# A two-layer streaming encoder: row tiles kept in one pool from the mixer to the next half-step, the embedding through the weight ring, raw buffers by stage, one down block reordered

## The chip, the cores and the metric

The kernel runs on one core of one Trainium2 chip. Its time is the time of one execution on the device in microseconds (us). The engines are named as in the profile: PE is the matrix engine (TensorE) and PEld its weight loads, DVE is VectorE, ACT is ScalarE, POOL is GpSimd, and SP only issues DMAs (its queue appears as SPq). PE runs at one of two clocks, 1.2 or 2.4 GHz; the profile gives the granted clock of a stretch as a share of the higher one.

## The reference, cut to what matters

The kernel computes two consecutive encoder layers on 512 tokens of width 1024, all in fp32. LN is a layer norm over the 1024 channels, alpha = (2*DEPTH)^(1/4).

```
for each of DEPTH = 2 layers:
  x <- LN(alpha*x + 0.5*SwiGLU_1(x))                      # first half-step, D_FF = 2816
  x <- LN(alpha*x + W_out(sum_b sigmoid(G_b x) * (W_b y_b)))   # four mixers y_A..y_D
  x <- LN(alpha*x + 0.5*SwiGLU_2(x) + sigmoid(x W_pg) * (p[i] W_p))   # second half-step + per-layer embedding

def swiglu(x, w_up, w_down):
    a, b = jnp.split(x @ w_up, 2, axis=-1)
    return (jax.nn.silu(a) * b) @ w_down
```

p[i] is an embedding of 256 numbers per token, one for each layer; the kernel gets it transposed, as pT.

## The kernel before, in words

The 512 tokens are four **row tiles** of 128 (i = 0 to 3, NT = 4). The running residual is z0 to z3, one [128, 1024] tile for each row tile; the operand of the matmuls is its transpose, which `norm` makes on PE (tiles lnT) and splits.

**Precision.** Every matmul is made of three passes (`mm3`, lines 163 to 165): each operand is split into a high part and a low rest (`split`, lines 177 and 178: ACT casts the high part, DVE subtracts it from the source). A "group" below is one `mm3`, three matmuls. A weight tile so needs four steps (`weights`): SP issues a DMA of 512 KB into a raw tile named `stage`, ACT casts `whi`, DVE subtracts `wlo`, and PE reads both. Finished pairs have six slots. Raw tiles come from `stage()`: four buffers in the pool `ring`, and four more in the pool `more` while the pool `tt` is open; `stage()` alternates between the two. `norm` takes raw tiles for its intermediate sums as well (`sums`).

**Stages of a layer.** The first half-step (`ffn`, which = 1) goes over 22 blocks of D_FF in four chunks (6, 6, 6 and 4). `unit` computes the up product of a block with seven products of block sums in place of eight; the operands of these are th and tl, which live in the pool `tt`. `down` then adds a chunk's blocks into z. Then `mix` runs the four mixers, gates and merges them into `mg`, multiplies by the output weights (tiles wo), adds to z and normalises. The second half-step (`ffn`, which = 2) begins with `ple`: for each half of the channels, pw = p times the embedding weights (wple) and pg = x times the gate's (wpg), then the same up and down loops. The last chunk's down product is `down_last`: for each row tile and each half of the channels it goes over the block pairs pr, and after each row tile a `norm` is spawned. The norm after `down_last` of the first half-step and the mixer's norm also write z to DRAM (`scratch`, tiles xs), from where the next stage loads it again.

**Order.** PE's order is written out by hand: generators such as `norm` are woven into the main stream at estimated times (`Weave`), and PE executes them in that order. On ACT, DVE and SP the scheduler decides the order; each engine then goes strictly through its own list. So an instruction that waits holds up all that stands behind it on its engine, and a DMA that waits holds up all DMAs behind it on SP's queue.

Of the kernel before, what the change touches and what calls it, by code (L numbers as in the profile page):

```python
# [9 lines left out]
F32 = mybir.dt.float32  # L10
F32R = mybir.dt.float32r
I32 = mybir.dt.int32
AF = mybir.ActivationFunctionType
ALU = mybir.AluOpType
# [4 lines left out]
P = 128  # L19
D = 1024  # L20
KD = D // P
SEQ = 512
NT = SEQ // P
DEPTH = 2
# [16 lines left out]
class Weave:  # L41
# [25 lines left out]
    def spawn(self, gen):  # L67
        c = Chain(gen)
        self.chains.append(c)
        self.step(c)  # L70
        return c
# [8 lines left out]
class Trunk:  # L80
# [14 lines left out]
    def __init__(self, tc, ctx, t):  # L95
        self.tc, self.nc, self.t = tc, tc.nc, t
        pool = lambda *a, **k: ctx.enter_context(tc.tile_pool(*a, **k))
        self.const = pool(name="const", bufs=1)
        self.ring = pool(name="ring", bufs=1)
        self.small = pool(name="small", bufs=4)  # L100
        self.dram = pool(name="dram", bufs=1, space=DRAM)
        self.psum = pool(name="psum", bufs=8, space=PSUM)
        c = self.const
        self.xh = c.tile([P, KD, SEQ], F32R, tag="xh", name="xh")
        self.xl = c.tile([P, KD, SEQ], F32R, tag="xl", name="xl")
        self.ident = c.tile([P, P], F32, tag="ident", name="ident")
        self.mhalf = c.tile([P, 8], F32, tag="mhalf", name="mhalf")
        self.st, self.ln = {}, []
        self.tt, self.turn = None, False
        self.scratch = [self.dram.tile([P, D], F32, tag=f"xs{i}", name=f"xs{i}") for i in range(NT)]  # L110
        self.w = Weave()

# [5 lines left out]

    def stage(self):
        self.turn = not self.turn  # L120
        if self.tt is not None and self.turn:
            return self.more.tile([P, 1024], F32, tag="stage", name="stage", bufs=4)
        return self.ring.tile([P, 1024], F32, tag="stage", name="stage", bufs=4)

# [127 lines left out]
        self.th, self.tl = [p.tile([P, 4, HK, HT], F32R, tag=q, name=q) for q in ("th", "tl")]  # L252

    def close_tt(self):
        self.tt.close()
        self.tt = None

    def xop(self, c):

# [116 lines left out]
            v.tensor_scalar(s, s, -1.0, 0.5 * math.pi, op0=ALU.mult, op1=ALU.add)  # L376
            nc.scalar.activation(self.cos, s, AF.Sin)

    def load_res(self, z, src):
        for i in range(NT):  # L380
            self.load(z[i], src[i])

    def load_gb(self, g, b, l, which):
        self.load(g, self.t[f"ln{which}_g"][l].partition_broadcast(P))
# [4 lines left out]
            self.st[i] = self.small.tile([P, 2, 6], F32, tag="st", name="st", bufs=5)  # L389
        self.nc.vector.bn_stats(self.st[i][:, half, :], z[:, half * 512:(half + 1) * 512])  # L390

    def norm(self, z, i, g, b, last, blocks):
        nc = self.nc
        mv = self.small.tile([P, 2], F32, tag="mv", name="mv")
        nc.vector.bn_aggr(mv, self.st[i])
# [7 lines left out]
                nc.sync.dma_start(out=self.t["out"][i][:, c], in_=z[:, c])  # L403
        if last:
            return
        self.load(self.scratch[i], z)
        for j in range(2):
            yield 8.5 if j == 0 else 1.0
            ps = self.bank("lnT", [P, 4, P])
            for q in range(4):  # L410
                k = 4 * j + q
# [27 lines left out]
            self.mm3(ps[:, c0:c1], w[0][:, s], w[1][:, s], self.xh[:, k, c0:c1], self.xl[:, k, c0:c1],  # L439
                     k == 0, k == KD - 1)  # L440

    def ffn(self, l, which, res, last):
        nc, t = self.nc, self.t
        v = nc.vector
        up, dn = t[f"up{which}"][l], t[f"dn{which}"][l]
        pool = lambda n: self.tc.tile_pool(name=f"{n}{l}{which}", bufs=1, reuse_waits="tile")
        with pool("z") as zp:
            first_use = l == 0 and which == 1
            if first_use:
                scratch = zp.tile([P, D], F32, tag="z3", name="trig")  # L450
            z = []

            def load_rows():
                z.extend(zp.tile([P, D], F32, tag=f"z{i}", name=f"z{i}") for i in range(NT))
                self.load_res(z, res)

            if not first_use:
                load_rows()
            if which == 2:
                with pool("ple") as pp:  # L460
                    self.ple(l, z, pp, self.load_p(l, pp))
            with pool("ffn") as fp:
                self.ffn_body(l, which, last, fp, z, up, dn, load_rows, scratch if first_use else None)

    def ffn_body(self, l, which, last, fp, z, up, dn, load_rows, scratch):
        nc, t = self.nc, self.t
        v = nc.vector
        lead = 2 if which == 1 else 0
        alpha = ALPHA2 if which == 1 else None
        h = {}  # L470
# [28 lines left out]
        def down_last(k0, k1, g, b):  # L499
            prs = range(k0 // 2, k1 // 2)  # L500
            ws = {(pr, half): self.weights(dn[pr, half]) for half in range(2) for pr in prs}
            self.ln = []
            for i in range(NT):
                for half in range(2):
                    ps = self.bank(f"dn{i}")
                    for pr in prs:
                        w = ws[pr, half]
                        for j in range(2):
                            s, m = slice(i * P, (i + 1) * P), slice(j * 512, (j + 1) * 512)
                            self.mm3(ps, h[pr][:, 0, j, s], h[pr][:, 1, j, s], w[0][:, m], w[1][:, m],  # L510
                                     2 * pr + j == k0, 2 * pr + j == k1 - 1)
                    zs = z[i][:, half * 512:(half + 1) * 512]
                    v.tensor_tensor(zs, zs, ps, op=ALU.add)
                    self.stats(z[i], i, half)
                self.ln.append(self.w.spawn(self.norm(z[i], i, g, b, last, which == 2)))

        for ci, (k0, k1) in enumerate(CHUNKS):
            first, tail = ci == 0, ci == len(CHUNKS) - 1
# [19 lines left out]
                g, b = gb[:, 0, :], gb[:, 1, :]  # L538
                self.load_gb(g, b, l, 1 if which == 1 else 3)
            while tt < k1:  # L540
                if scratch is not None and tt == lead + 2:
                    self.constants(scratch)
                    load_rows()
                self.ready(*range(NT))
                cc, X, nb = self.unit(up[tt // 2], fp)
                finish(tt // 2, cc, (X, nb))
                tt += 2
# [11 lines left out]
            self.nc.vector.tensor_tensor(cc[:, q], cc[:, q], ps[2 * q + 1], op=ALU.mult)  # L559
        self.split(h[0][:, 0], h[0][:, 1], cc)  # L560

    def load_p(self, l, pp):
        ps_ = pp.tile([P, 2, SEQ], F32, tag="ps", name="ps_")
        ph = pp.tile([P, 2, SEQ], F32R, tag="ph", name="ph")
        pl = pp.tile([P, 2, SEQ], F32R, tag="pl", name="pl")
        self.load(ps_, self.t["pT"][l])
        self.split(ph, pl, ps_)
        return ph, pl

    def ple(self, l, z, pp, pt):  # L570
        nc, t = self.nc, self.t
        ph, pl = pt
        for half in range(2):
            wp = self.weights(t["wple"][l, half])
            pws = []
            for i in range(NT):
                s = slice(i * P, (i + 1) * P)
                pw = self.bank("pw")
                for k in range(2):
                    m = slice(k * 512, (k + 1) * 512)  # L580
                    self.mm3(pw, ph[:, k, s], pl[:, k, s], wp[0][:, m], wp[1][:, m], k == 0, k == 1)
                pws.append(pw)
            for i, pg in self.tok_proj("pg", t["wpg"][l, :, half], 512):
                tg = pp.tile([P, 512], F32, tag="tg", name="tg", bufs=2)
                nc.scalar.activation(tg, pg, AF.Tanh, scale=0.5)
                nc.vector.scalar_tensor_tensor(tg, tg, 1.0, pws[i], op0=ALU.add, op1=ALU.mult)
                zs = z[i][:, half * 512:(half + 1) * 512]
                nc.vector.scalar_tensor_tensor(zs, zs, ALPHA2, tg, op0=ALU.mult, op1=ALU.add)
# [31 lines left out]
        sl = (slice(None), slice(0, 2), slice(i * P, (i + 1) * P))  # L620
        self.split(y[0][sl], y[1][sl], ps)

    def mix(self, l, res):
        nc, t, tc = self.nc, self.t, self.tc
        spawn, need = self.w.spawn, self.w.need
        with ExitStack() as outer:
# [30 lines left out]
            with tc.tile_pool(name=f"chain{l}", bufs=1, reuse_waits="tile") as cp:  # L657
# [12 lines left out]
                branch(1, y1)  # L670
                need(c3[0])
                need(*c3[1])
            with tc.tile_pool(name=f"tailz{l}", bufs=1, side="right", reuse_waits="tile") as zp, \
                    tc.tile_pool(name=f"tail{l}", bufs=1, side="right", reuse_waits="tile") as mp:
                mg = mp.tile([P, 2, KD, SEQ], F32R, tag="mg", name="mg")
                z = [zp.tile([P, D], F32, tag=f"z{i}", name=f"z{i}") for i in range(NT)]
                g, b_ = [zp.tile([P, D], F32, tag=q, name=q) for q in ("lng", "lnb")]
                self.load_res(z, res)
                self.load_gb(g, b_, l, 2)
                branch(3, y3, mg)  # L680
                op_.close()
# [1 line left out]
                for half in range(2):  # L683
# [21 lines left out]
                    for i in range(NT):  # L705
                        for pr in late:
                            mm(pr, ws[pr], i)
                        add(i)
                        if half:
                            self.ln.append(spawn(self.norm(z[i], i, g, b_, False, True)))  # L710

    def mla(self, l, cp, y):
        nc, t = self.nc, self.t
# [292 lines left out]
        return cs  # L1006

    def run(self):
        res = [self.t["x"][i] for i in range(NT)]
        with self.tc.manual_schedule(engines={mybir.EngineType.PE}):  # L1010
            self.open_tt()
            for l in range(DEPTH):
                self.ffn(l, 1, res, False)
                self.close_tt()
                res = self.scratch
                self.mix(l, res)
                self.ffn(l, 2, res, l == DEPTH - 1)
            self.close_tt()


# [26 lines left out]
def layout(a):  # L1047
    a = {k: np.asarray(v) for k, v in a.items()}
    L = DEPTH
    o = {}  # L1050
    x = a["x"].reshape(SEQ, D)
    o["x"] = x.reshape(NT, P, D)
    o["xT"] = x.reshape(SEQ, KD, P).transpose(2, 1, 0)
    o["pT"] = a["p"].reshape(L, SEQ, 2, P).transpose(0, 3, 2, 1)
    o["pos"] = a["positions"].reshape(NT, P).T

    def stat(w, nm):
# [53 lines left out]
```

## Time and profile before

| what | value |
|---|---|
| median of 3 runs | 2414.93 us (2413.49 to 2416.49) |
| the profiled execution's own time | 2415.43 us |
| span of its trace | 2413.7 us |
| PE busy | 2355.1 us, 98% |
| DVE busy | 1570.3 us, 65% |
| ACT busy | 906.7 us, 38% |
| mean granted clock of PE | 0.988 |
| moved by DMA | 257.66 MB, 106 GB/s over the span |

The span is the stretch between the first and last record of the trace; 1.7 us of the execution lie outside it. The median is that of other executions than the profiled one, which is 0.5 us above it. Busy time of PE counts a matmul at half clock as busy all the same, so the share alone doesn't tell all of what is lost.

### The profile page before, as it was taken

To read this page: it belongs to the slowest core of one execution; us is meant where nothing else is said; L and a number is where in the kernel's file an instruction comes from. 1 tells how busy PE (TensorE), PEld (TensorE's weight loads), DVE (VectorE), ACT (ScalarE), POOL (GpSimd) and SP (SyncE) were. 2 spreads that over 40 slices of the span, in tenths; PEclk is the share of its full clock that TensorE was granted. 3 is DMA by queue.
4 is the path that set the end of the run, shared out by engine and by line. 5 is a ranking of instruction groups with operands and counts; after the bars stand their busy time and mean duration, and the time that the engine had idled before them with its cause. 6 is when DMAs were issued, how large, how long until landed. Compare 5 with 4: busy or idle time off the path is not lost.

```text
span 2413.7 us, 33826 instructions
## 1 busy us (share of the span) xinstructions
PE 2355.1 (98%) x14020; PEld 2072.3 (86%) x14020; DVE 1570.3 (65%) x2228; ACT 906.7 (38%) x1198; POOL 55.4 (2%) x93
## 2 busy tenths in 40 slices
PE   9999999999998799999999999999999988999998
PEld 8899887888887598998898998878888866989987
DVE  8777588545445675776796775885454466767757
ACT  6344344233222343433353443342332213534432
POOL 0000001000000000000000000010000000000000
PEclk9999999999999899999999999999999998999999
DMA  6333324222422523423253333242224224323331
GB/s 203 127 118 99 111 97 126 71 88 79 140 70 70 183 92 101 123 79 120 74 178 102 114 105 106 94 124 75 88 79 139 80 96 157 106 82 119 99 111 44
DMA packets 76969, 257.66 MB, mean 107 GB/s; under 512 B 10384, under 2 KB 13584, under 8 KB 76816
## 3 DMA queue, kind: packets, MB, share of 16 engines
q1 hardware_dynamic: 76816, 255.51, 33.0%
q8 instruction: 110, 1.80, 0.3%
q14 instruction: 43, 0.35, 0.0%
HBM read 242.89 MB, written 12.58 MB: 106 GB/s over the span
## 4 chain that ended last, share of the span: by engine, by line
PE 96%; DVE 3%; DMA 1%; ACT 1%; issue 0%; SPq 0%; DVEq 0%; ACTq 0%
PE dn L164 7%; PE dn L165 7%; PE dn L163 7%; PE sX L163 6%; PE sX L165 6%; PE sX L164 6%; PE gate L165 5%; PE gate L164 5%; PE gate L163 5%; PE sY L163 3%; PE sY L165 3%; PE sY L164 3%; PE sZ L164 2%; PE sZ L165 2%; PE sZ L163 2%; PE pg L163 1%
## 5 line engine op out<-in xcount | busy, mean ns | idle before, releaser
L178 DVE TENSOR_TENSOR wlo<-stage,whi 128x1024 fp32r<-128x1024 f32 (+2 forms) x558 | 661.6, 1191 | 426.9 <-ACT whi L177 426.3
L177 ACT CAST whi<-stage 128x1024 fp32r<-128x1024 f32 (+2 forms) x558 | 568.7, 1026 | 599.9 <-PE dn L165 316.2
L163 PE MATMUL dn<-wlo,hp 128*128 128x512 f32 x704 | 280.2, 398 | 2.7 <-ACT hp L177 2.7
L164 PE MATMUL dn<-whi,hp 128*128 128x512 f32 x704 | 279.2, 397 | 3.6 <-DVE hp L178 3.6
L163 PE MATMUL sX<-tl,whi 128*128 128x256 f32 x1008 | 282.2, 280 | 0.4 <-DVE nb L284 0.4
L164 PE MATMUL sX<-th,wlo 128*128 128x256 f32 x1008 | 281.2, 279 | 0.9 <-DVE wlo L178 0.9
L165 PE MATMUL sX<-th,whi 128*128 128x256 f32 x1008 | 281.3, 279 | 0.0
L165 PE MATMUL dn<-whi,hp 128*128 128x512 f32 x704 | 279.0, 396 | 0.0
L138 DVE TENSOR_TENSOR stage<-stage 128x1024 f32<-128x1024 f32 x168 | 204.6, 1218 | 9.2 <-DMA stage<-up_in 7.7
L163 PE MATMUL gate<-xl,whi 128*128 128x512 f32 x512 | 206.0, 402 | 0.0
L165 PE MATMUL gate<-xh,whi 128*128 128x512 f32 x512 | 202.6, 396 | 0.0
L164 PE MATMUL gate<-xh,wlo 128*128 128x512 f32 x512 | 202.6, 396 | 0.0
L164 PEld LDWEIGHTS sX<-th,wlo 128*128 128x128 f32 x1008 | 188.9, 187 | 1.3 <-DVE wlo L178 1.3
L163 PEld LDWEIGHTS sX<-tl,whi 128*128 128x128 f32 x1008 | 189.1, 188 | 0.6 <-issue 0.6
L165 PEld LDWEIGHTS sX<-th,whi 128*128 128x128 f32 x1008 | 189.4, 188 | 0.0
L164 PEld LDWEIGHTS dn<-whi,hp 128*128 128x128 f32 x704 | 132.6, 188 | 36.1 <-DVE hp L178 4.9
L163 PEld LDWEIGHTS dn<-wlo,hp 128*128 128x128 f32 x704 | 132.7, 188 | 35.7 <-ACT hp L177 4.4
L165 PEld LDWEIGHTS dn<-whi,hp 128*128 128x128 f32 x704 | 132.5, 188 | 32.6
L642 ACT ACTIVATE gate<-gate 128x512 f32<-128x512 f32 x64 | 38.2, 597 | 234.7 <-PE gate L165 212.4
L165 PEld LDWEIGHTS gate<-xh,whi 128*128 128x128 f32 x512 | 96.2, 188 | 23.0
L164 PEld LDWEIGHTS gate<-xh,wlo 128*128 128x128 f32 x512 | 96.3, 188 | 21.4 <-DVE wlo L178 0.2
L163 PEld LDWEIGHTS gate<-xl,whi 128*128 128x128 f32 x512 | 96.4, 188 | 21.0
(305 smaller groups left out, 4798.7 us busy)
## 6 DMA issues: line engine op xcount, KB each, us to landing
stage<-up_in SPq DMA_DIRECT2D x172, 512.0 KB, 3.9
stage<-dn_in SPq DMA_DIRECT2D x88, 512.0 KB, 3.6
stage<-wg_in SPq DMA_DIRECT2D x64, 512.0 KB, 3.8
xs<-z SPq DMA_DIRECT2D x20, 512.0 KB, 2.6
z<-xs SPq DMA_DIRECT2D x20, 512.0 KB, 5.6
stage<-wbr_in SPq DMA_DIRECT2D x16, 512.0 KB, 3.8
stage<-wo_in SPq DMA_DIRECT2D x16, 512.0 KB, 3.7
stage<-wpg_in SPq DMA_DIRECT2D x16, 512.0 KB, 5.9
```

The lines of the kernel that those rows point to most:

```text
L138: add = lambda o, x, y: self.nc.vector.tensor_tensor(o, x, y, op=ALU.add)
L163: mm(ps, lh, rl, start=start, stop=False, **more)
L164: mm(ps, ll, rh, start=False, stop=False, **more)
L165: mm(ps, lh, rh, start=False, stop=stop, **more)
L177: self.nc.scalar.copy(hi, src)
L178: self.nc.vector.tensor_tensor(lo, src, hi.bitcast(F32), op=ALU.subtract)
L642: nc.scalar.activation(tg, ps, AF.Tanh, scale=0.5)
```

## The change

There are four edits. (1) A pool `rows` on the right side of the memory holds z0 to z3. It is opened at the start and again at the end of `mix`, and stays open through the second half-step and the next layer's first half-step; so the stores to scratch behind the mixer's norm and the second half-step's norm are gone, and the loads behind them (12 of 20 stores, 12 of the 24 loads of z). Only the first half-step's norm stores (`keep`). (2) pT is loaded through the weight ring, once for each half in `ple`, instead of into tiles of its own at the start of `ffn`; this is one more load of 512 KB, with its cast and subtract, in each layer. (3) A flag `wide` replaces "the pool `tt` is open" in `stage()`: the four raw buffers of `more` are used only in `ffn_body`, so the wo loads, the sums of the mixer's norm and all of `ple` go through the four of `ring`. (4) `down_last` takes the first row tile's work by pr first and half second; the other row tiles keep half first.

```diff
     def stage(self):
         self.turn = not self.turn
-        if self.tt is not None and self.turn:
+        if self.wide and self.turn:
             return self.more.tile([P, 1024], F32, tag="stage", name="stage", bufs=4)
...
+    def open_rows(self):
+        self.rows = ExitStack()
+        p = self.rows.enter_context(self.tc.tile_pool(name="rows", bufs=1, side="right", reuse_waits="tile"))
+        self.z = [p.tile([P, D], F32, tag=f"z{i}", name=f"z{i}") for i in range(NT)]
...
-        self.load(self.scratch[i], z)
+        if keep:
+            self.load(self.scratch[i], z)
...
+    def ffn(self, l, which, last):
+        pool = lambda n: self.tc.tile_pool(name=f"{n}{l}{which}", bufs=1, reuse_waits="tile")
+        if which == 2:
+            with pool("ple") as pp:
+                self.ple(l, self.z, pp)
+        self.wide = True
+        with pool("ffn") as fp:
+            self.ffn_body(l, which, last, fp, self.z)
...
-                for half in range(2):
-                    ps = self.bank(f"dn{i}")
-                    for pr in prs:
+                order = [(half, pr) for half in range(2) for pr in prs]
+                if i == 0:
+                    order.sort(key=lambda x: x[1])
...
-    def load_p(self, l, pp):
-        ps_ = pp.tile([P, 2, SEQ], F32, tag="ps", name="ps_")
...
-        self.load(ps_, self.t["pT"][l])
-        self.split(ph, pl, ps_)
...
         for half in range(2):
+            ph, pl = [q.rearrange("p (k n) -> p k n", k=2) for q in self.weights(t["pT"][l])]
             wp = self.weights(t["wple"][l, half])
```

PE's order is the same in both but for edit (4). Three places on the other engines show what moved.

On SP, from the output weights of layer 0 to the first gate weights of `ple`; xs are the tiles in DRAM, z the row tiles, ps_ the tile of pT. Before:

```order
L132 DMA stage<-wo_in 128x1024 x8
L132 DMA stage<-wple_in 128x1024
L181 DMA xs_73<-z_6087 128x1024
L181 DMA xs_74<-z_6088 128x1024
L181 DMA xs_75<-z_6089 128x1024
L181 DMA z_6818<-xs_73 128x1024
L181 DMA z_6819<-xs_74 128x1024
L181 DMA z_6820<-xs_75 128x1024
L181 DMA xs_76<-z_6090 128x1024
L181 DMA ps__6829<-pT_in 128x1024
L181 DMA z_6821<-xs_76 128x1024
L132 DMA stage<-wpg_in 128x1024 x4
```

And with the change:

```order
L132 DMA stage<-wo_in 128x1024 x8
L132 DMA stage<-pT_in 128x1024
L132 DMA stage<-wple_in 128x1024
L181 DMA stage<-up_in 128x1024 x4
L132 DMA stage<-wpg_in 128x1024 x4
L132 DMA stage<-pT_in 128x1024
```

The stores and loads of z are gone, pT has come in front of wple, and loads of the half-step's first up weights now stand ahead of the gate weights.

On DVE, the end of the norm of row tile 2 in layer 0 (its sums are the rows of lines 244 to 246 and from 421 to 433) and the subtracts of the first four wpg tiles. Before:

```order
L178 TENSOR_TENSOR tl<-stage,th 128x4x128
L246 SCALAR_TENSOR_TENSOR stage<-stage,xh 128x512
L178 TENSOR_TENSOR tl<-stage,th 128x4x128
L427 TENSOR_TENSOR stage<-stage,xl 128x512
L178 TENSOR_TENSOR tl<-stage,th 128x4x128
L178 TENSOR_TENSOR wlo<-stage,whi 128x1024
L178 TENSOR_TENSOR tl<-stage,th 128x4x128
```

And with the change:

```order
L178 TENSOR_TENSOR tl<-stage,th 128x4x128
L246 SCALAR_TENSOR_TENSOR stage<-stage,xh 128x512
L178 TENSOR_TENSOR tl<-stage,th 128x4x128
L433 TENSOR_TENSOR stage<-stage,xl 128x512
L178 TENSOR_TENSOR tl<-stage,th 128x4x128 x2
L178 TENSOR_TENSOR wlo<-stage,whi 128x1024 x4
```

The first wpg tile's subtract stood ahead of the norm's last tl and now stands behind it; apart from that the piece is the same.

On ACT, the last merges of the four mixers in layer 0 (mg, four row tiles) and the casts of the output weights. Before:

```order
L177 CAST mg<-acc_4518 128x512
L642 ACTIVATE gate<-gate 128x512
L177 CAST mg<-acc_4566 128x512
L642 ACTIVATE gate<-gate 128x512
L177 CAST mg<-acc_4608 128x512
L642 ACTIVATE gate<-gate 128x512
L177 CAST mg<-acc_4650 128x512
L642 ACTIVATE gate<-gate 128x512
L177 CAST mg<-acc_4692 128x512
L177 CAST whi<-stage 128x1024 x9
```

And with the change:

```order
L177 CAST whi<-stage 128x1024
L177 CAST mg<-acc_4565 128x512
L632 ACTIVATE gate<-gate 128x512
L177 CAST whi<-stage 128x1024
L177 CAST mg<-acc_4607 128x512
L632 ACTIVATE gate<-gate 128x512
L177 CAST whi<-stage 128x1024
L177 CAST mg<-acc_4649 128x512
L632 ACTIVATE gate<-gate 128x512
L177 CAST whi<-stage 128x1024 x2
L177 CAST mg<-acc_4691 128x512
L177 CAST whi<-stage 128x1024 x4
```

All nine casts (eight of wo, one of wple) stood behind the last mg; now five of the nine casts shown stand ahead of it, each as soon as its raw tile may land.

## Rows read from the trace of the kernel before

**Rows 1.** Page, part 1: engine, busy us, share of the span, instructions

```profile
PE 2355.1 (98%) x14020; PEld 2072.3 (86%) x14020; DVE 1570.3 (65%) x2228; ACT 906.7 (38%) x1198; POOL 55.4 (2%) x93
```

**Rows 2.** Waits of PE: line, releaser, us in total, times, longest

```profile
PE pw L163 <- ACT ph L177: 22.0, 2, 11.4
PE pg L163 <- DVE wlo L178: 12.3, 2, 6.1
PE wo L163 <- DVE wlo L178: 4.4, 1, 4.4
PE dn L164 <- DVE hp L178: 3.6, 4, 1.0
```

**Rows 3.** Timeline of SP's queue, layer 0: start, us, issue

```profile
786.73 0.43 SPq L181 DMA_DIRECT2D ps__6829<-pT_in  x1
790.60 2.90 SPq L132 DMA_DIRECT2D stage<-wpg_in  x4
```

**Rows 4.** Timeline of PE around `ple`: start, us, matmul, [idle before <-releaser]

```profile
780.95 0.40 PE L163 MATMUL wo<-wlo,mg 128*128 128x512 f32 x1
793.19 0.79 PE L163 MATMUL pw<-wlo,ph 128*128 128x512 f32 x1 [11.37 <-ACT ph L177]
...
815.72 0.60 PE L173 MATMUL lnT<-ident,z 128*128 128x128 f32 x4
816.07 0.47 PE L163 MATMUL pg<-wlo,xh 128*128 128x512 f32 x1
...
816.84 0.40 PE L163 MATMUL pg<-wlo,xh 128*128 128x512 f32 x1
...
817.55 0.39 PE L163 MATMUL pg<-wlo,xh 128*128 128x512 f32 x1
...
1981.54 0.40 PE L163 MATMUL wo<-wlo,mg 128*128 128x512 f32 x1
...
2017.72 0.39 PE L163 MATMUL pg<-wlo,xh 128*128 128x512 f32 x1
```

**Rows 5.** Windows: us; busy of PE, PEld, DVE, ACT, POOL; clock, DMA share, GB/s

```profile
809.30:813.20 3.90, 3.88 (x10) 3.08 (x11) 3.88 (x4) 1.62 (x2) 0.00 (x0) 0.52 0.83 290
```

**Rows 6.** Timeline of PE at the start of wo, layer 0

```profile
727.30 0.39 PE L163 MATMUL br<-y,whi 128*128 128x512 f32 x1
...
732.58 0.79 PE L163 MATMUL wo<-wlo,mg 128*128 128x512 f32 x1 [4.43 <-DVE wlo L178]
...
738.60 0.39 PE L163 MATMUL wo<-wlo,mg 128*128 128x512 f32 x1
```

**Rows 7.** Timeline of DVE around `ple`, layer 0

```profile
784.94 1.41 DVE L401 SCALAR_TENSOR_TENSOR z<-z,rsln,lnb 128x512 f32<-128x512 f32 x2
...
806.15 0.68 DVE L178 TENSOR_TENSOR tl<-stage,th 128x512 fp32r<-128x512 f32 x1
...
807.96 1.22 DVE L178 TENSOR_TENSOR wlo<-stage,whi 128x1024 fp32r<-128x1024 f32 x1
```

**Rows 8.** Timeline of ACT around `ple`, layer 0

```profile
804.99 1.04 ACT L177 CAST whi<-stage 128x1024 fp32r<-128x1024 f32 x1
```

**Rows 9.** DMA issues: KB each, median us to landing

```profile
stage<-wpg_in SPq DMA_DIRECT2D x16, 512.0 KB, 5.9
```

**Rows 10.** Timelines of PE and DVE at the start of `down_last`

```profile
329.49 0.39 PE L163 MATMUL dn<-wlo,hp 128*128 128x512 f32 x1
...
333.81 0.39 PE L163 MATMUL dn<-wlo,hp 128*128 128x512 f32 x1
...
331.96 1.22 DVE L178 TENSOR_TENSOR hp<-cc,hp 128x1024 fp32r<-128x1024 f32 x1
...
1181.07 0.39 PE L163 MATMUL dn<-wlo,hp 128*128 128x512 f32 x1
...
1189.03 0.39 PE L163 MATMUL dn<-wlo,hp 128*128 128x512 f32 x1
...
2381.25 0.39 PE L163 MATMUL dn<-wlo,hp 128*128 128x512 f32 x1
...
2385.16 0.39 PE L163 MATMUL dn<-wlo,hp 128*128 128x512 f32 x1
```

More of the change, by code (lines that the diff above doesn't have):

```diff
@@ L108, in __init__ @@
         self.st, self.ln = {}, []
-        self.tt, self.turn = None, False
+        self.tt, self.turn, self.wide = None, False, False
         self.scratch = [self.dram.tile([P, D], F32, tag=f"xs{i}", name=f"xs{i}") for i in range(NT)]
@@ L254, in close_tt @@
     def close_tt(self):
+        self.wide = False
         self.tt.close()
-        self.tt = None
+    def open_rows(self):
+        self.rows = ExitStack()
+        p = self.rows.enter_context(self.tc.tile_pool(name="rows", bufs=1, side="right", reuse_waits="tile"))
+        self.z = [p.tile([P, D], F32, tag=f"z{i}", name=f"z{i}") for i in range(NT)]
     def xop(self, c):
@@ L377, in trig, with load_rows @@
             nc.scalar.activation(self.cos, s, AF.Sin)
-    def load_res(self, z, src):
+    def load_rows(self, src):
         for i in range(NT):
-            self.load(z[i], src[i])
+            self.load(self.z[i], src[i])
     def load_gb(self, g, b, l, which):
@@ L390, in stats, with norm @@
         self.nc.vector.bn_stats(self.st[i][:, half, :], z[:, half * 512:(half + 1) * 512])
-    def norm(self, z, i, g, b, last, blocks):
+    def norm(self, z, i, g, b, last, blocks, keep):
         nc = self.nc
@@ L440, in up_mm, with ffn_body @@
                      k == 0, k == KD - 1)
-    def ffn(self, l, which, res, last):
+    def ffn(self, l, which, last):
[6 more added lines that the diff above has]
+            self.ffn_body(l, which, last, fp, self.z)
+    def ffn_body(self, l, which, last, fp, z):
         nc, t = self.nc, self.t
@@ L445, in ffn @@
         up, dn = t[f"up{which}"][l], t[f"dn{which}"][l]
[L446 to L467, printed above, removed]
         lead = 2 if which == 1 else 0
@@ L503, in down_last @@
             for i in range(NT):
-                for half in range(2):
-                    ps = self.bank(f"dn{i}")
-                    for pr in prs:
[L507 to L515, printed above, removed]
+                order = [(half, pr) for half in range(2) for pr in prs]
+                if i == 0:
+                    order.sort(key=lambda x: x[1])
+                ps = {}
+                for half, pr in order:
+                    if pr == prs[0]:
+                        ps[half] = self.bank(f"dn{i}")
+                    w = ws[pr, half]
+                    for j in range(2):
+                        s, m = slice(i * P, (i + 1) * P), slice(j * 512, (j + 1) * 512)
+                        self.mm3(ps[half], h[pr][:, 0, j, s], h[pr][:, 1, j, s], w[0][:, m], w[1][:, m],
+                                 2 * pr + j == k0, 2 * pr + j == k1 - 1)
+                    if pr == prs[-1]:
+                        zs = z[i][:, half * 512:(half + 1) * 512]
+                        v.tensor_tensor(zs, zs, ps[half], op=ALU.add)
+                        self.stats(z[i], i, half)
+                self.ln.append(self.w.spawn(self.norm(z[i], i, g, b, last, which == 2, which == 1)))
         for ci, (k0, k1) in enumerate(CHUNKS):
@@ L540, in ffn_body @@
             while tt < k1:
-                if scratch is not None and tt == lead + 2:
-                    self.constants(scratch)
-                    load_rows()
+                if l == 0 and which == 1 and tt == lead + 2:
+                    self.constants(z[3])
+                    self.load_rows(t["x"])
                 self.ready(*range(NT))
@@ L560, in lead, with ple @@
         self.split(h[0][:, 0], h[0][:, 1], cc)
-    def load_p(self, l, pp):
-        ps_ = pp.tile([P, 2, SEQ], F32, tag="ps", name="ps_")
-        ph = pp.tile([P, 2, SEQ], F32R, tag="ph", name="ph")
-        pl = pp.tile([P, 2, SEQ], F32R, tag="pl", name="pl")
-        self.load(ps_, self.t["pT"][l])
-        self.split(ph, pl, ps_)
-        return ph, pl
-    def ple(self, l, z, pp, pt):
+    def ple(self, l, z, pp):
         nc, t = self.nc, self.t
-        ph, pl = pt
         for half in range(2):
+            ph, pl = [q.rearrange("p (k n) -> p k n", k=2) for q in self.weights(t["pT"][l])]
             wp = self.weights(t["wple"][l, half])
@@ L621, in to_feature, with mix @@
         self.split(y[0][sl], y[1][sl], ps)
-    def mix(self, l, res):
+    def mix(self, l):
         nc, t, tc = self.nc, self.t, self.tc
@@ L672, in mix @@
                 need(*c3[1])
-            with tc.tile_pool(name=f"tailz{l}", bufs=1, side="right", reuse_waits="tile") as zp, \
-                    tc.tile_pool(name=f"tail{l}", bufs=1, side="right", reuse_waits="tile") as mp:
+            self.open_rows()
+            z = self.z
+            with tc.tile_pool(name=f"tail{l}", bufs=1, side="right", reuse_waits="tile") as mp:
                 mg = mp.tile([P, 2, KD, SEQ], F32R, tag="mg", name="mg")
-                z = [zp.tile([P, D], F32, tag=f"z{i}", name=f"z{i}") for i in range(NT)]
-                g, b_ = [zp.tile([P, D], F32, tag=q, name=q) for q in ("lng", "lnb")]
-                self.load_res(z, res)
+                g, b_ = [mp.tile([P, D], F32, tag=q, name=q) for q in ("lng", "lnb")]
+                self.load_rows(self.scratch)
                 self.load_gb(g, b_, l, 2)
@@ L709, in mix @@
                         if half:
-                            self.ln.append(spawn(self.norm(z[i], i, g, b_, False, True)))
+                            self.ln.append(spawn(self.norm(z[i], i, g, b_, False, True, False)))
     def mla(self, l, cp, y):
@@ L1008, in run @@
     def run(self):
-        res = [self.t["x"][i] for i in range(NT)]
         with self.tc.manual_schedule(engines={mybir.EngineType.PE}):
             self.open_tt()
+            self.open_rows()
             for l in range(DEPTH):
-                self.ffn(l, 1, res, False)
+                self.ffn(l, 1, False)
                 self.close_tt()
-                res = self.scratch
-                self.mix(l, res)
-                self.ffn(l, 2, res, l == DEPTH - 1)
+                self.rows.close()
+                self.mix(l)
+                self.ffn(l, 2, l == DEPTH - 1)
+            self.rows.close()
             self.close_tt()
@@ L1053, in layout @@
     o["xT"] = x.reshape(SEQ, KD, P).transpose(2, 1, 0)
-    o["pT"] = a["p"].reshape(L, SEQ, 2, P).transpose(0, 3, 2, 1)
+    o["pT"] = a["p"].reshape(L, SEQ, 2, P).transpose(0, 3, 2, 1).reshape(L, P, 2 * SEQ)
     o["pos"] = a["positions"].reshape(NT, P).T
```

## The prediction

> **What bounds the kernel now.** I read the busy times of the page first: PE is busy for 98% of the span, the next engine, DVE, for 65% [rows 1]. So time can only come from PE: from gaps, from half clock (which counts as busy), or from fewer matmuls. The change takes no matmul away. The second view is therefore what PE waits for [rows 2]: five lines carry nearly all of its idle time, pw 22.0 us in 2 waits, pg 12.3 in 2, wo 4.4 in one, and the last down chunk, 3.6 in 4 (on DVE alone). All are places that the diff touches. The third view, PE's timeline, shows that each gap costs more than itself: after pg's wait of 6.1 us the next 3.90 us ran at a granted clock of 0.52, that is at 1.2 in place of 2.4 GHz [rows 2, 5].
>
> So I price every place by the distance between two matmuls, less what lies between them fully packed. A group (three matmuls) takes 0.71 us, 816.84 to 817.55, and four transposes 0.35, 815.72 to 816.07 [rows 4]; I use 0.70 and 0.36.
>
> **The change part by part.**
>
> *Start of wo, layer 0.* From br's last group but one (727.30) to wo's sixth group (738.60) is 11.30 us [rows 6]. Packed it would be six groups, 4.20 us, so 7.1 are lost: 4.43 idle, the rest half clock. The cause: wo's casts stand on ACT behind the last mg cast. In the changed order the first ones stand ahead of it, so PE has its operands when br ends. Gain **7.1**; at least 4.4 (the idle alone, if a shorter gap still slows the clock), at most 7.1. In layer 1 the waits have no such row, and I book nothing.
>
> *Start of ple.* Now pT's load stands on SP behind stores of z that wait for the norm of row tile 3; it is issued at 786.73 [rows 3], and PE, done with wo at 781.65, starts pw at 793.19 after 11.37 idle [rows 4]. Then pg waits 6.1 more [rows 2], because wpg's loads are issued even later (790.60 [rows 3]) and its subtract stands on DVE among the steps of norm 2. From wo's last group (780.95) to pg's ninth group (817.55) is 36.60 us in layer 0, and 36.18 in layer 1 (1981.54 to 2017.72) [rows 4]. Between them lie 17 groups and four sets of transposes, 17 x 0.70 + 4 x 0.36 = 13.3. Lost: 23.3 and 22.9. Of the first, 11.4 + 6.1 = 17.5 are idle and 5.8 are two restarts at half clock, 2.9 each.
>
> With the change pT's load has only wo's loads ahead of it, so pw starts at once, at 781.65. Eight pw groups and two sets of transposes later, at 781.65 + 5.6 + 0.7 = 787.96, PE wants pg. Its first subtract is late: on DVE norm 3's normalise ends at 784.94 + 1.41 = 786.35, then come 12 steps of norm 2 at 0.60 each (806.15 to 807.96 are three such steps) [rows 7], 7.2 us, to 793.6; the order puts the first wlo behind all of them. Its cast on ACT takes 1.04 [rows 8] and stands behind the last cast of th, then wlo 1.22 [rows 7]: 795.9. So a new wait of **8.0** us takes the place of two, between 6.9 (if the cast is done beside the chain: 793.6 + 1.22) and 8.8 (if the chain itself has waits as long as one step). It is between the two waits of before, 6.1 and 11.4, after both of which the clock fell; so I add a restart of 2.9 (2.5 by wo's: 738.60 less 732.58 less 3.50 [rows 6]).
>
> *Raw buffers.* In ple only the four of `ring` are left. In turn they hold pT, wple, two sums of norm 2; then wpg's four tiles take the buffers of pT, wple and the two sums. The last two wpg loads so wait for norm 2's last tl, 793.6. They land 5.9 later [rows 9], and cast and subtract give 801.8. PE wants the third tile after four groups and a set of transposes: at 799.1 if all run at full clock (795.9 + 2.80 + 0.36), and some 1.7 later, at 800.8, if three of the groups run at half clock. So PE waits between nothing (if the loads land sooner) and 2.7; I take **1.0**, since the half clock is the likelier. The second half's loads find their buffers earlier: its last wlo comes near 826.3, and PE wants it near 831; that cover of 4.8 us is what makes the second half free.
>
> New loss per layer 8.0 + 2.9 + 1.0 = 11.9. Gain 23.3 - 11.9 = 11.4 and 22.9 - 11.9 = 11.0, together **22.4**. Bounds: loss of 6.9 + 2.5 = 9.4 to 8.8 + 2.9 + 2.7 = 14.4 a layer, gain 17.4 to 27.4.
>
> Here a rule speaks against the change. The trace shows pg's present waits released by wlo, not by a missing buffer [rows 2]. The Trainium skill, Perfetto Trace Analysis, Optimization Strategy, says that the same gap repeating on the engine that should be saturated can mean that there isn't enough SBUF or PSUM for the next tile to be allocated; the change halves the raw buffers where PE already has gaps. By the row the sum is the one below; by the rule it is that of the last rival. No trace of the kernel before can show which, since it has eight buffers there.
>
> *The last down chunk.* Four times (two half-steps, two layers) the third group waits for hp, whose rest DVE has ready at 331.96 + 1.22 = 333.18 [rows 10]. From the first group to the fourth, 329.49 to 333.81, are 4.32 us for 2.10 packed: 2.2 lost. At 1181.07 the clock fell too: six groups, 4.20 us, took 7.96, 3.8 lost; the third place repeats that, and the fourth (2381.25 to 2385.16) loses 1.8 [rows 10]. Sum 11.5. With pr first, four groups of row tile 0 need no new hp, so PE reaches it at 329.49 + 2.80 + 0.23 = 332.52 and waits 0.7 (0.3 at the fourth place): 2.5 in all. Gain **9.1**; 6.0 if the clock falls in two places still.
>
> *The rest at nothing.* The stores and loads of z that go away, 24 x 512 KB, lie beside work of PE: no wait of rows 2 but pw's hangs on them, and this is booked. The extra pT load with its cast (1.04) and subtract (1.22) lies in the second half's cover of 4.8 us named above; without the cover it would cost at most 2.3 a layer. Up loads that now stand ahead of wpg on SP go to the buffers of `more`, free then; if the first of them had to wait, wpg would wait with it, which belongs to the second rival.
>
> Sum: 7.1 + 22.4 + 9.1 = 38.6. The profiled execution took 2415.43, 0.5 above the median of the runs; 2415.43 - 38.6 = **2376.8**. With every bound at its worse end (4.4 + 17.4 + 6.0 = 27.8) it is 2387.6, at its better end (7.1 + 27.4 + 11.5, if no hp wait were left) 2369.4.
>
> **The rivals.** A difference of 0.2%, 4.8 us, is about what a measurement of this kernel can tell from no change.
>
> - *No wait at pg.* If the casts and subtracts of wpg in fact came ahead of norm 2's steps, the 8.0, the restart and the 1.0 would go too: 2376.8 - 2 x 11.9 = 2353.0. For it: DVE has room, 65%. Against: the order on DVE as written, and engines go through it strictly. Chance 0.05.
> - *The ring starves PE a second time.* If the third wpg tile is 2.7 late and the clock falls again for it, each layer loses 1.7 + 2.9 more: 2386.0. For it: the loads wait for sums of a norm. Against: three slow groups of pg give the load time. Chance 0.08.
> - *It doesn't do what it says.* If pT's load were as late as before, for want of a ring buffer while wo's tiles hold them, only wo and the down chunk gain: 2415.4 - 16.2 = 2399.2. Against: wo's tiles are read long before 781. Chance 0.03.
> - *Four buffers serialise the loads: slower.* If in ple each load waited for the tile before it to be read out (one in flight), a turn would be 5.9 + 1.04 + 1.22 = 8.2 us [rows 7 to 9], and the 12 loads of ple 98.4, where PE now needs 80.7 for them (80 groups, 1.4 of transposes and the 23.3 lost). Then each layer is 17.7 longer: 2415.4 + 35.4 - 16.2 = 2434.6. It decides from a turn of 7.4 us, at which 12 turns (88.8) eat the other 8.1 a layer as well. Against: four buffers allow four in flight, so the turn would have to be four times as long. Chance 0.03 for slower, and 0.02 for a turn that ends near no change.
>
> **How the numbers follow.** The forecast has 0.79 and is 2376.8, with its own range of 2370 to 2385. The range given, 2368 to 2388, takes in its bounds and the starved ring, and leaves out the other three rivals (0.05 + 0.03 + 0.05) and some of the forecast's own tails, under 0.2. Faster by over 0.2%: 0.79 + 0.05 + 0.08 + 0.03 = 0.95; within 0.2%: 0.02; slower 0.03.
>
> **What would show it.** PE's waits of the changed kernel: no row for wo on wlo and none for pw on the cast of ph; a row for pg of some 16 to 18 us in a few waits, released by wlo; dn on hp with some 2.5 us in 4. The stretch behind pg's start has a granted clock near 0.5, and the start of wo near 1. On DVE the first wlo of wpg stands behind the last tl of norm 2, at about 14 us after wo's end. The prediction is wrong if pw waits still, if pg's waits repeat with every wpg tile, or if waits appear at up or wo, where none is booked.

## The result, and the profile after

The changed kernel takes 2373.04 us (median of 4 runs, 2371.32 to 2373.45) against 2415.71 us for the kernel before (4 runs, 2413.49 to 2417.49): a ratio of 0.9822, 95% interval 0.9805 to 0.9839. The forecast was 2376.8, so it is 3.8 us faster than forecast, inside the range. The span of the profiled execution went from 2413.7 to 2371.6 us, 42.1 less.

The waits of PE after the change (columns as in [rows 2]):

```profile
PE pg L163 <- DVE wlo L178: 15.8, 2, 7.9
PE up L163 <- DVE xl L178: 1.7, 1, 1.7
PE dn L164 <- DVE hp L178: 1.6, 3, 0.5
```

The three lines that led [rows 2] have changed: pw and wo are gone, and pg has grown from 12.3 to 15.8. That is the new wait in place of two that the prediction names, 7.9 for the 8.0 forecast. The wait of up is not new: the kernel before has it too, with the same 1.7 us in one. PE's timeline around the embedding in both layers, to be read against [rows 4] (the first row of each layer is wo's last group, the last one pg's ninth):

```profile
772.41 0.40 PE L163 MATMUL wo<-wlo,mg 128*128 128x512 f32 x1
...
773.11 0.39 PE L163 MATMUL pw<-wlo,whi 128*128 128x512 f32 x1
...
787.59 0.77 PE L163 MATMUL pg<-wlo,xh 128*128 128x512 f32 x1 [7.92 <-DVE wlo L178]
...
796.12 0.39 PE L163 MATMUL pg<-wlo,xh 128*128 128x512 f32 x1
...
1953.30 0.40 PE L163 MATMUL wo<-wlo,mg 128*128 128x512 f32 x1
...
1977.06 0.39 PE L163 MATMUL pg<-wlo,xh 128*128 128x512 f32 x1
```

The distance that was 36.60 is now 23.71, and the one that was 36.18 is 23.76: 12.9 and 12.4 gained. pw begins 0.70 behind wo's last group, one group's time, so nothing is lost there. Behind pg's wait the clock is at half again, and it is full at the start of wo, where it was half (windows, columns as in [rows 5]; the first two are the start of wo, before and after, the third is pg's start after):

```profile
732.58:736.50 3.92, 3.92 (x9) 3.14 (x10) 3.15 (x3) 2.80 (x3) 0.00 (x0) 0.50 0.96 298
...
726.50:731.00 4.50, 4.50 (x21) 3.60 (x21) 4.16 (x5) 2.04 (x3) 0.00 (x0) 1.00 0.20 81
...
787.60:791.50 3.90, 3.90 (x9) 3.10 (x10) 2.20 (x2) 1.67 (x2) 0.00 (x0) 0.50 0.39 149
```

The timelines of DVE and ACT show why pg waits. On DVE the first row ends norm 3's normalise, the second is the last two tl of norm 2, the third the first two subtracts of wpg; the ACT row is the casts of these two wpg tiles:

```profile
776.40 1.41 DVE L406 SCALAR_TENSOR_TENSOR z<-z,rsln,lnb 128x512 f32<-128x512 f32 x2
...
784.50 1.46 DVE L178 TENSOR_TENSOR tl<-stage,th 128x512 fp32r<-128x512 f32 x2
786.22 2.36 DVE L178 TENSOR_TENSOR wlo<-stage,whi 128x1024 fp32r<-128x1024 f32 x2 [0.25 <-ACT whi L177]
```

```profile
785.14 1.99 ACT L177 CAST whi<-stage 128x1024 fp32r<-128x1024 f32 x2
```

The last tl ends at 785.96 and the first subtract near 787.4; PE starts at 787.59. wo ends where pw begins, at 773.11, so the first subtract ends 14.3 us behind it, where the prediction named about 14.

The other two places, wo in layer 0 (from br's last group but one to wo's sixth group, as [rows 6]) and the first of the four last down chunks (its first and sixth group, as [rows 10]):

```profile
725.87 0.39 PE L163 MATMUL br<-y,whi 128*128 128x512 f32 x1
...
730.06 0.40 PE L163 MATMUL wo<-wlo,mg 128*128 128x512 f32 x1
...
329.47 0.39 PE L163 MATMUL dn<-wlo,hp 128*128 128x512 f32 x1
...
333.21 0.51 PE L164 MATMUL dn<-whi,hp 128*128 128x512 f32 x1 [0.55 <-DVE hp L178]
...
333.79 0.39 PE L163 MATMUL dn<-wlo,hp 128*128 128x512 f32 x1
```

To wo's sixth group it is now 4.19 in place of 11.30. In the down chunk five groups take 4.32 for 3.50 packed: 0.8 lost where it was 2.2. The second and third place read the same, and the fourth has no wait on hp left and loses 0.4.

### The profile page after: what moved, and what is told of

Read it like the earlier page. It is cut to its first block, busy times and chain, and to the rows that moved or that the text cites. A ratio compares the mean times of both kernels' runs of the same rounds, so it can differ in the third digit from the quotient of the medians.

```text
span 2371.6 us, 33791 instructions
## 1 busy us (share of the span) xinstructions
PE 2341.6 (99%) x14020; PEld 2065.3 (87%) x14020; DVE 1572.1 (66%) x2230; ACT 908.7 (38%) x1200; POOL 55.3 (2%) x93
## 4 chain that ended last, share of the span: by engine, by line
PE 95%; DVE 3%; issue 1%; ACT 1%; DMA 0%; SPq 0%; DVEq 0%; ACTq 0%
PE dn L164 7%; PE dn L165 7%; PE dn L163 7%; PE sX L163 6%; PE sX L165 6%; PE sX L164 6%; PE gate L165 5%; PE gate L163 5%; PE gate L164 5%; PE sY L163 3%; PE sY L165 3%; PE sY L164 3%; PE sZ L164 2%; PE sZ L165 2%; PE sZ L163 2%; PE pg L163 1%
```

## The experiments

All times are medians; each version was timed beside the kernel before, whose median lay between 2414.8 and 2417.1 in these runs. Each version leaves out one edit of the change or alters one resource or one order. The intervals of the ratios reach some 3 to 4 us to either side, so they barely tell the smallest differences below, 3.8 and 4.5 us, from none; these rest on the waits in the traces, and on the single runs, which do not overlap with those of the change (at least 2374.8 against at most 2373.5).

**Without edit 4** (the old order of the first row tile's down block):

```diff
                 order = [(half, pr) for half in range(2) for pr in prs]
-                if i == 0:
-                    order.sort(key=lambda x: x[1])
```

> The change without the reordered down block. If the waits on hp are what the reorder shortens, each of the four last down chunks loses again what it gained (1.5, 3.0, 2.4 and 1.5 us by the two traces), so the time is 2373.0 + 8.5 = 2381.5 us, PE's waits show dn on hp four times on ACT and four times on DVE, and nothing else moves. If those gains came from elsewhere (buffers or transfers that the other edits freed), the time stays within 2 us of 2373.0.

Measured: 2379.47 us, 6.4 above the change; ratio to before 0.9850 (0.9837 to 0.9864). The waits on hp are back, four on ACT (2.7) and four on DVE (3.6), and pg stays at 15.9. Of the 8.5 expected 2.1 are missing, and the trace shows most of them: in the kernel before the clock fell after the second and the third of these places, here only after the second, so the third loses 2.2 in place of some 3.8. The rest is not assigned. Two windows, the second place and the third:

```profile
1164.80:1168.20 3.40, 3.40 (x11) 2.60 (x10) 1.38 (x2) 0.00 (x0) 0.00 (x0) 0.52 0.00 0
1518.60:1522.00 3.40, 3.40 (x17) 2.72 (x16) 1.38 (x2) 0.00 (x0) 0.00 (x0) 1.00 0.29 114
```

The waits ahead of both are alike (0.72 on ACT, 0.95 on DVE), so the same program and the same waits were followed by either clock.

**Without edit 3** (eight raw buffers in wo and the embedding, four in `ring` and four in `more`):

```diff
-        if self.wide and self.turn:
+        if self.tt is not None and self.turn:
```

> The change with eight raw buffers in the output weights and the embedding, as before, in place of four. If the start of wo is won by edit 3, because casts of tiles in the second pool stand behind the mixers' merges on ACT, the wait of wo on wlo is back with 4.4 us and 7.0 us in all, and the pg wait is 1 us shorter in each layer (one subtract now stands one step earlier): about 2373.0 + 7.0 - 2 = 2378 us. If the start of wo is won by the rows' pool or the pT load instead, no wait of wo is back: 2371 us or the same. If four raw buffers starve PE, eight make it faster: below 2370 us with no wait for wpg at all.

Measured: 2377.49 us (0.9841, 0.9828 to 0.9854), as expected by the theory. PE's waits:

```profile
PE pg L163 <- DVE wlo L178: 13.6, 2, 6.8
PE wo L163 <- DVE wlo L178: 4.4, 1, 4.4
```

The wait at wo is back in full, and pg's is 1.1 shorter in each layer. So edit 3, not the rows' pool, wins the start of wo; and four raw buffers don't starve the embedding, since eight shorten pg's wait only by about what the other place of one subtract gives. SP and PE in layer 0 show besides that the loads are not what pg waits for:

```profile
736.09 11.10 SPq L132 DMA_DIRECT2D stage<-wpg_in  x4
```

```profile
793.04 0.77 PE L163 MATMUL pg<-wlo,xh 128*128 128x512 f32 x1 [6.81 <-DVE wlo L178]
```

All four wpg loads are issued by 747.2 here, and pg still waits, until 793.0. The trace of SP fits the start of wo as well: here the last five wo loads of layer 0 are issued over 29.69 us, to 729.6, and with the change over 21.27, to 722.0. That the four tiles of `more` come free late because they lie in memory that the mixers held is what I take for the reason; no run shows it.

**Without edit 2** (pT in tiles of its own, once a layer):

```diff
-                self.ple(l, self.z, pp)
+                self.ple(l, self.z, pp, self.load_p(l, pp))
...
+    def load_p(self, l, pp):
+        ps_ = pp.tile([P, 2 * SEQ], F32, tag="ps", name="ps_")
+        ph = pp.tile([P, 2 * SEQ], F32R, tag="ph", name="ph")
+        pl = pp.tile([P, 2 * SEQ], F32R, tag="pl", name="pl")
+        self.load(ps_, self.t["pT"][l])
+        self.split(ph, pl, ps_)
```

> The change, but with pT in tiles of its own as before, loaded once a layer at the start of the second half-step. If pw started late only because pT's load stood behind the stores of z, keeping the rows is enough: no wait of pw, pg waits as with the change, 2373 us within 4. If the way through the weight ring is what brings pT early, pw waits again by up to 11 us a layer: about 2395 us.

Measured: 2388.8 us (0.9889, 0.9875 to 0.9902). This was a miss: with the stores of z gone, pw still waits 9.6 us in two, and 15.8 us of the gain are lost. pT's load on SP and its cast on ACT in layer 0:

```profile
772.26 0.33 SPq L181 DMA_DIRECT2D ps__6812<-pT_in  x1
```

```profile
776.09 1.04 ACT L177 CAST ph<-ps__6812 128x1024 fp32r<-128x1024 f32 x1 [4.63 <-DMA ps__6812<-pT_in]
```

Nothing of z stands ahead of it on SP, yet it is issued only at 772.26, about when the last wo matmul has run (wo's last group starts at 771.37 in that trace). My theory that the stores ahead of it were the whole cause had fallen.

**pT's raw tile from the ring, its split in own tiles.** The next run asks whether the late load is what is left:

```diff
-        ps_ = pp.tile([P, 2 * SEQ], F32, tag="ps", name="ps_")
+        ps_ = self.stage()
```

> As the version with pT in tiles of its own, but its raw tile comes from the ring, so that its load is issued early, behind wo's loads; only the high and low parts are tiles of their own. If the load's late issue was the whole cause there (its raw tile lies where the mixers' merge lay, which wo's last matmul still reads), no wait is left at pw but that for the cast, 1 to 1.5 us, and the time is about 2379 us. If it was one of two limits, the cast still waits for wo's last matmul and the low part's subtract stands on DVE behind norm 3's normalise, which ends near 777.8: pw's first pass waits 1.3 us, its second some 4 us, and the time is that of tiles of its own again, 2386 to 2389 us.

Measured: 2387.29 us (0.9887, 0.9871 to 0.9904): the load is now issued at 727.78, 44 us earlier, and the time is that of own tiles again. The rows of three engines show two limits behind the load: ACT's cast, then DVE, where pl's subtract stands behind norm 3's normalise, then PE's two waits:

```profile
772.41 1.04 ACT L177 CAST ph<-stage 128x1024 fp32r<-128x1024 f32 x1 [0.81 <-PE wo L165]
```

```profile
775.50 1.41 DVE L406 SCALAR_TENSOR_TENSOR z<-z,rsln,lnb 128x512 f32<-128x512 f32 x2
776.83 1.22 DVE L178 TENSOR_TENSOR pl<-stage,ph 128x1024 fp32r<-128x1024 f32 x1
```

```profile
773.51 0.51 PE L163 MATMUL pw<-wlo,ph 128*128 128x512 f32 x1 [1.13 <-ACT ph L177]
778.10 0.80 PE L164 MATMUL pw<-whi,pl 128*128 128x512 f32 x1 [4.08 <-DVE pl L178]
```

The cast is released by wo's matmuls, which I read as ph lying in memory that wo's operands held; and pl stands on DVE behind norm 3's normalise. In the ring's slots, which the change uses, neither holds: with the change all casts and subtracts of pT and wple are done by 752.2, some 20 us ahead of wo's end.

**Without edit 1**, in two ways. The first stores every norm's z and loads it back into the same tiles:

```diff
+        if which == 2 or l > 0:
+            self.load_rows(self.scratch)
```

> The change, but every norm stores its row tile to scratch and the next stage loads it again, as before; pT still goes through the weight ring. If pT's place on SP decides, pw starts at once here too, and only wpg's loads, which stand behind the stores and loads of z, are late: they can be issued some 4 us later than with the change, so the pg wait grows from 7.9 to about 12 us in each layer: 2381 us. If the stores and loads themselves cost time (traffic, queue), it is more than that, up to 2396 us; if they are hidden, 2373 us.

Measured: 2380.93 us (0.9855, 0.9841 to 0.9869), the number expected, but for another reason: since the reload overwrites the tile that norm transposes, lnT waits for it (7.9 us in 3, also at the end of layer 0, where neither kernel has a wait), and pg's wait is shorter, 7.3. This version brings a wait of its own, so I don't read the edit's price from it. The second way is the kernel before with edits 2, 3 and 4, and z reloaded into other tiles, as there:

```diff
-        if self.tt is not None and self.turn:
+        if self.wide and self.turn:
...
-                    self.ple(l, z, pp, self.load_p(l, pp))
+                    self.ple(l, z, pp)
+            self.wide = True
...
+            ph, pl = [q.rearrange("p (k n) -> p k n", k=2) for q in self.weights(t["pT"][l])]
```

> The kernel before with edits 2, 3 and 4 and without the rows' pool: z is stored behind the mixer's norm and loaded again into other tiles, pT goes through the ring ahead of these transfers on SP. pw starts at once. wpg's four loads stand behind the last store and load of z, so they are issued near 782 and land near 788 in layer 0, against a need at 785.1; pg starts some 2 us later than with the change in each layer: 2377 us. If the transfers of z cost more than their place on SP (traffic that slows the weights), it is over 2381; if they are hidden, 2373.

Measured: 2376.85 us (0.9841, 0.9828 to 0.9854), 3.8 above the change. pw doesn't wait; pg's longest wait is 9.9:

```profile
781.79 0.32 SPq L181 DMA_DIRECT2D z<-xs  x1
782.17 3.96 SPq L132 DMA_DIRECT2D stage<-wpg_in  x4
```

```profile
789.33 0.77 PE L163 MATMUL pg<-wlo,xh 128*128 128x512 f32 x1 [9.86 <-DVE wlo L178]
```

wpg's loads stand behind the last load of z, as in [rows 3], and the cast of the first waits for its landing. pg's waits are 2.9 longer in all (18.7 against 15.8); that is most of what the 12 stores and 12 loads cost, and no other wait that the trace shows grows by more than 0.6.

**Two raw buffers in the embedding.** This is the slower rival's mechanism, made real:

```diff
-        return self.ring.tile([P, 1024], F32, tag="stage", name="stage", bufs=4)
+        self.side = not self.side and not self.thin
+        return self.ring.tile([P, 1024], F32, tag="stage1" if self.side else "stage", name="stage", bufs=2)
...
+            self.thin = True
             with pool("ple") as pp:
                 self.ple(l, self.z, pp)
+            self.thin = False
```

> The change with two of the four raw buffers used in the embedding (and by the sums of its norms). Then all four wpg tiles wait for the last step of norm 2 near 786: the first is ready at 786 + 0.3 + 3.7 + 1.04 + 1.22 = 792.2, so the pg wait grows from 7.9 to 12.5, and the third and fourth come a turn of 6 us later, a second wait of some 2 to 5 us: 7 us in each layer, about 2388 us. If raw buffers don't matter in this stretch, 2373; if the loads serialise in the second half too, over 2400.

Measured: 2385.11 us (0.9876, 0.9862 to 0.9889), 12.1 above the change, against 15 expected. The first wait has the size that was expected, 12.3 us in place of 7.9; the later ones, at the later wpg tiles, are smaller than the 2 to 5 us expected:

```profile
791.63 0.76 PE L165 MATMUL pg<-wlo,xh 128*128 128x512 f32 x1 [12.26 <-DVE wlo L180]
797.47 0.50 PE L165 MATMUL pg<-wlo,xh 128*128 128x512 f32 x1 [0.58 <-DVE wlo L180]
```

So raw buffers do bind in this stretch at two, and don't at four.

**Early wpg, a better version.** The loads of the first half's wpg are asked for ahead of pw in the program, which puts their casts and subtracts ahead of the norms' steps on ACT and DVE:

```diff
             pws = []
+            early = [self.weights(t["wpg"][l, pr, half]) for pr in range(4)] if half == 0 else None
...
-            for i, pg in self.tok_proj("pg", t["wpg"][l, :, half], 512):
+            for i, pg in self.tok_proj("pg", t["wpg"][l, :, half], 512, early):
...
-    def tok_proj(self, name, src, n):
-        ws = [self.weights(src[pr], 2 * n) for pr in range(4)]
+    def tok_proj(self, name, src, n, ws=None):
+        ws = ws or [self.weights(src[pr], 2 * n) for pr in range(4)]
```

> The change, with the first half's four wpg tiles asked for ahead of pw's matmuls in the program instead of behind them. If pg waits only because the subtracts of wpg stand on DVE behind the steps of norm 2, these now stand ahead of norm 3's steps, no wait of pg is left and the restart behind it goes too: 7.9 + 2.1 in each layer, 2373.0 - 20 = 2353 us. If wpg's own arrival (raw buffers, slots held by the output weights until 773) is a second limit close behind, PE waits for it at pg or pw: 2358 to 2368 us.

Measured: 2352.49 us; ratio to before 0.9743 (0.9729 to 0.9756), 20.6 us below the change. No wait of pg is left in either layer. PE at the seam between pw and pg, DVE's four subtracts and a window over the stretch:

```profile
779.15 0.39 PE L163 MATMUL pw<-wlo,whi 128*128 128x512 f32 x1
779.84 0.40 PE L163 MATMUL pg<-wlo,xh 128*128 128x512 f32 x1
```

```profile
772.22 1.22 DVE L178 TENSOR_TENSOR wlo<-stage,whi 128x1024 fp32r<-128x1024 f32 x1
...
777.57 1.17 DVE L178 TENSOR_TENSOR wlo<-stage,whi 128x1024 fp32r<-128x1024 f32 x1
```

```profile
773.00:800.00 27.00, 27.00 (x126) 21.98 (x125) 26.78 (x43) 13.48 (x22) 0.99 (x1) 1.00 0.23 72
```

The subtracts that ended at 787.4 and later now end by 778.7, PE never stops there and its clock stays at 1.00. DVE is busy for 26.78 of the 27.00 us: the work was not made less, it was put in the order in which PE wants it. The last of the four subtracts ends 1.1 us ahead of pg's start.

**Early wpg, and the sums of the mixer's norm in the second pool's raw tiles:**

```diff
-                t = self.sums(HK)
+                t = self.sums(HK, not keep)
...
-        a, b = [self.stage().rearrange("p (c k n) -> p c k n", c=2, k=nk) for _ in range(2)]
+        a, b = [(self.spare if spare else self.stage)().rearrange("p (c k n) -> p c k n", c=2, k=nk) for _ in range(2)]
```

> The same, and the sums of the mixer's norm take raw tiles of the second pool, so that the four of the ring hold only weights in the embedding. If four raw buffers are enough for that, the time is that of the version with early wpg alone, within 2 us; if the sums are what holds the third and fourth wpg tile back, it is up to 10 us faster than that version.

Measured: 2354.46 us (0.9750, 0.9736 to 0.9763), not told apart from early wpg alone. Four raw buffers are enough in this order.

## Why the prediction was right, point by point

| term | forecast | measured by the same rows |
|---|---|---|
| start of wo, layer 0 | 7.1 | 7.1 (11.30 less 4.19) |
| embedding, layer 0 | 11.4 | 12.9 (36.60 less 23.71) |
| embedding, layer 1 | 11.0 | 12.4 (36.18 less 23.76) |
| last down chunks | 9.1 | 8.7 (11.5 lost before, 2.8 now) |
| sum | 38.6 | 41.1, of 42.1 in the span |

- **What bounds it.** The four lines of [rows 2] and dn's wait on ACT (2.7 us in 4, the fifth line that the prediction counts) were the change's whole field; the measured gains lie at these places but for 1.0 us, which I leave unassigned.
- **Start of wo.** Right in size; the run with eight raw buffers shows that edit 3 is its cause. That the order on ACT changes along with it is what the prediction read from the order.
- **The new pg wait.** Right in mechanism: the cast and subtract behind norm 2's steps. Early wpg takes that order away, and the whole loss of some 10 us a layer goes with it; it asks for the loads earlier too, but with eight raw buffers they were early and pg waited all the same. That the size came so near (8.0 forecast, 7.9 measured) is in part luck: from the end of norm 3's normalise to norm 2's last tl it took 8.2 us (777.81 to 785.96) for the 7.2 forecast, and the subtract ended only 1.4 behind that for the 2.3 forecast, because the cast ran beside the last tl. These are the conditions that the prediction names for its two bounds; both came, and nearly cancel.
- **The restart of 2.9** was too large. By the rule that gave it (all that is lost, less the idle time) it is 23.71 less 13.3 less 7.9, or 2.5; from PE's start at 787.59 to the ninth pg group alone are 8.53 us for 6.32 packed, 2.2 lost. I had averaged two restarts of before, and the one behind the wait of 11.4 us was the longer; it also held a wait for pl of 0.47.
- **The 1.0 us for the raw buffers** was nothing. I took 5.9 us from issue to landing [rows 9]; with the change a wpg load lands in a median of 4.0 us. The last of the four subtracts ends at 793.2, and PE needs it only at its seventh pg group, at 794.6. With the restart that is some 1.4 us a layer, and with the 0.1 of the wait 1.5: the 2.9 us by which the embedding of both layers was forecast too low.
- **Last down chunks.** Right within 0.4. The forecast took the clock to stay full there, and it did. By its own terms (11.5 less 2.5) the forecast is 9.0, not 9.1.
- **Why pw had waited.** Here the prediction named one cause, the stores of z ahead of pT's load on SP [rows 3], and there were three in a row: SP's queue; behind it the memory, which wo's matmuls still read; behind that pl's place on DVE. With the first taken away PE still waited 4.95 us for ph, and with the load early as well 1.13 for ph and 4.08 for pl. So edit 2 does the work at pw, since the ring's slots and place pass by all three, and edit 1, which I had credited with it as well, is worth some 3.8 us, mostly at pg.
- **The rule against the change.** With two raw buffers in the embedding pg waits at later wpg tiles as well, 26.9 us in 6. At four and at eight there is one gap a layer, and early wpg closed it without a buffer more. The Trainium skill, Perfetto Trace Analysis, Optimization Strategy, says that the same gap repeating on the engine that should be saturated can mean too little SBUF for the next tile. The trace with two buffers agrees with that; the gap at four and at eight is not of that kind.
- **The rivals.** "No wait at pg" didn't come, but it was the right description of early wpg: 2353.0 worked out there, 2352.5 measured. The ring didn't starve PE a second time, and the loads didn't serialise.

Leaving out one edit each costs 3.8 (edit 1), 15.8 (edit 2), 4.5 (edit 3) and 6.4 us (edit 4), 30.5 of the 42.7 that all four bring. The rest I put down to edits 1 and 2 in common, because with only one of them undone pT's load still doesn't stand behind the stores; no run undoes just these two.

## What to carry to other kernels

When PE waits for an operand, follow the operand past the first thing that holds it: what queue its DMA stands in, what memory its tile takes over, and where its cast and subtract stand on engines that execute in order; removing the first limit alone can leave much of the wait (4.95 of 11.37 us here, 2388.8 against 2373.0). When the engine that feeds PE is late though it has idle time elsewhere, look at the order on it before adding buffers: early wpg, worth 20.6 us, only moved four tiles' loads, casts and subtracts ahead of steps that PE did not yet need. A gap that is to be closed is worth more than itself if the clock falls behind it: here 10.3 us a layer for a wait of 7.9.

## What was not expected of the hardware

After single idle times of 4.4 us and more PE ran at a granted clock of 0.50 to 0.52 at once in all stretches looked at but one, and 2.2 us were lost behind the 7.9. The exception is layer 1 of the version with pT in tiles of its own: the first matmul behind 4.63 us of idle time took 0.51 us, where the others took 0.76 to 0.80, and only from the next, 1.26 us later, the clock stood at 0.50:

```profile
1964.96 0.51 PE L163 MATMUL pw<-wlo,ph 128*128 128x512 f32 x1 [4.63 <-ACT ph L177]
1966.22 0.79 PE L164 MATMUL pw<-whi,pl 128*128 128x512 f32 x1 [0.76 <-DVE pl L178]
```

After two short waits close together, 0.72 and 0.95 us at the first three places and 0.5 and 0.8 at the fourth, the clock fell at two of the four in the kernel before and at one of the four in the version without edit 4: some 3.8 us lost or 2.2 at one and the same place, behind the same waits. After the 0.55 that the reordered chunk leaves it stayed full at all three places.
